# SyncE's transfers in the planner's order, and a table load that the planner counts

## The chip, the core and the metric

The kernel runs on one core of one Trainium2 chip. The core has five engines that run side by side: TensorE (PE in the profile) multiplies matrices, VectorE (DVE) and ScalarE (ACT) do elementwise work, GpSimd (POOL) does some elementwise work and issues accumulating transfers, and SyncE (SP) issues nearly all other transfers. Each engine works through its own list of instructions in order and waits on semaphores for the others. The metric is the device time of one execution in microseconds (us); less is better.

## The reference

Two layers of a decoder trunk work on one sequence of 512 tokens, with 16 learned tokens put ahead of it, so on 528 rows of width 1024, all in float32. Each layer has two halves, and each half is normalised before and after:

```python
for l in range(DEPTH):                      # DEPTH = 2
    u = rms_norm(h, mix_pre_g[l])
    z = u @ w_in[l]                         # q, k, v, forget gate, two conv groups
    y = concat(forgetting_attention(...),   # 8 heads of 64, causal, with a decay F[t] - F[s]
               conformer_conv(...),         # 31 taps, layer norm, silu, a pointwise matmul
               short_conv(...))             # 3 taps
    h += rms_norm(head_rms_norm(y) @ w_out[l], mix_post_g[l])
    u = rms_norm(h, ffn_pre_g[l])
    g, up = split(conv3(u @ w_up[l]))       # each 2816 wide, 3 taps along the sequence
    h += rms_norm((silu(g) * up) @ w_down[l], ffn_post_g[l])
return h[:, 16:]
```

## The kernel before, in words

**Layout.** Activations lie transposed: 128 channels on the partitions, 8 channel tiles (KD), 528 columns of sequence in two halves of 264. The last layer drops the first 16 columns, so most of its tiles are 512 wide in the FFN. To keep float32 accuracy every operand is split into a high and a low part (names ending in hi and lo), and each product is three matmuls: hi x hi, hi x lo, lo x hi (mm3, line 659 on, whose matmul is line 668; line 709 in the class First, lines 1204 and 1462 in the attention stages, line 2198 in the FFN).

**Weights** come in blocks through a ring of three raw buffers. For one block SyncE loads it (load in plan_block, line 604), ScalarE writes the high part (high, line 608), VectorE writes the low part (low, line 612), and then the raw buffer is free for the next load. In the FFN load_op (line 2061) loads the blocks of w_up into the buffers g and u, line 2336 those of w_down into draw and raw, and lines 2049 and 2052 split them.

**Stages of a layer.** The mixer (line 894) makes q, k, v and the convolution inputs, and runs the attention of head after head; small transfers by dma (line 535) copy rows of q and k and the gate rows of the heads (gate_rows, line 1270: from an SBUF tile for heads 0 to 3, from g_dram for heads 4 to 7). Then finish (line 1642) makes w_out, the norm and the addition to h; load_h (line 490) brings h back from DRAM for it. Then comes the FFN: 22 pairs of tiles f (NF), the first six by plain products, the other 16 by seven products in place of eight (class Seven, line 2066), whose operand sums GpSimd makes by accumulating transfers (line 2086). h is stored to h_mid for that time (line 1901). Each pair is filtered by three taps (conv_flow, line 2115), the gate half goes through silu (line 2151), the two are multiplied and split again (gate_flow, lines 2164, 2171 and 2175), and w_down is accumulated in five parts (downs, line 2318; the last part again by finish). Tile 21 is the last one, and the last part of w_down needs it last.

**What sets the order.** A planner written into the kernel (class Flow, line 247) decides it while the program is built. Each operation is given to it as engine, estimated duration, priority (lower goes first) and what it waits for; TensorE's work is given as threads. Flow.run (line 308) goes forward in estimated time: on each engine, among the operations that are ready by the time that it is free, the one of the lowest priority goes, and when an operation's turn comes, its instructions are emitted. An operation counts as ready 0.06 us (HOP) after what it waits for. So the planner has an order for every engine, SyncE among them ("sp" operations). In the program it holds only for the engines that manual_schedule names (the set every, line 1784): TensorE, ScalarE, VectorE and GpSimd. SyncE is left out of the set, and its transfers are put in order by the framework's own scheduler, which runs a simulated timeline over the program (the kernel is built with schedule_with_timeline_sim=True) and may take a transfer before others that were emitted earlier.

Priorities that matter here: the taps, silu and split of tile f have 1.5 + 0.001 f (conv_prio), the copies out of PSUM 0, blocks of w_up and w_down in the FFN about 1 + 0.001 f (part 0 of w_down 0.7 and 0.9, the plain blocks 0.5), the blocks of plan_block 2 unless something else is given, and the loads of h for the last finish of a layer 3, not before a time:

```python
plan_w(len(chunks) if final else after_mixer[l + 1])
h, h_at = load_h(fp, h_mid[l], prio=3, after_all=[Tok(flow.now + 4)])
```

**The table load.** ScalarE evaluates functions from tables. silu needs another set than the exponentials and logarithms of the norms and of the attention, so behind the last silu of a layer (f == NF - 1) the kernel loads the set EXPSET again (line 2154). In the planner the silu has act_us(n) = 0.17 + 0.0009 n us, and the table load nothing: it is emitted inside the silu's operation.

Of the kernel before, what the change touches and what calls it, by code (L numbers as in the profile page):

```python
# [26 lines left out]
NF = DFF // P  # L27
# [336 lines left out]
def act_us(n):  # L364
    return 0.17 + 0.0009 * n
# [6 lines left out]
def stt_us(n):  # L372
    return 0.22 + 0.00102 * n
# [13 lines left out]
def tile_hybrid_trunk(ctx: ExitStack, tc: tile.TileContext, xT, wflat, pv_d, out):  # L387
    nc = tc.nc
# [3 lines left out]
    def T(pool, shape, dt, tag, bufs=None):  # L392
        uid[0] += 1
        kw = {} if bufs is None else {"bufs": bufs}
        return pool.tile(list(shape), dt, tag=tag, name=f"{tag}_{uid[0]}", **kw)
# [4 lines left out]
    PE, ACT = mybir.EngineType.PE, mybir.EngineType.Activation  # L400
    DVE, POOL = mybir.EngineType.DVE, mybir.EngineType.Pool
# [67 lines left out]
    EXPSET = "natural_log_exp_and_others"  # L469
# [55 lines left out]
    def act(us, fn, *after, **kw):  # L525
        return flow.op("act", us, fn, after, **kw)

    def dve(us, fn, *after, **kw):
        return flow.op("dve", us, fn, after, **kw)

    def gp(us, fn, *after, **kw):
        return flow.op("pool", us, fn, after, **kw)
# [1248 lines left out]
    after_first = [next(i for i, c in enumerate(chunks) if c[0] == "ffn_w_up" and c[1] == l) + FIRST["w_out"] + 3  # L1781
                   for l in range(DEPTH)]
    after_down = next(i for i, c in enumerate(chunks) if c[1] == 1) + FIRST["ffn_w_down"]
    every = {PE, ACT, DVE, POOL}
    with tc.tile_pool(name="pre", bufs=2, reuse_waits="tile") as sp, tc.manual_schedule(engines=every):
        h, h_at = load_h(sp, xT, also=[(0, 2)], prios=OH)
        act(1.3, lambda: nc.scalar.preload_act_table_set(EXPSET), prio=-2)
# [21 lines left out]
    for l in range(DEPTH):  # L1809
        pv, pg = pvs[l]  # L1810
        final = l == DEPTH - 1
# [19 lines left out]
        with tc.tile_pool(name=f"fp{l}", bufs=2, reuse_waits="tile") as fp:  # L1831
# [47 lines left out]
            def wtap(i, t):  # L1879
                c = _COLS["ffn_w"] + 3 * t + i  # L1880
                return pv[:, c:c + 1]

            def z_of(f, e):
                return zs[(2 * f + e) % len(zs)]
# [159 lines left out]
            def split_op(box, name, raw, after, bufs, slot, n, prio):  # L2044


                def high():
                    box[name] = [t[:, :n] for t in bufs.get(slot)]
                    nc.scalar.copy(box[name][0], raw())  # L2049

                a = act(act_us(n), high, *after, prio=prio, takes=[(bufs.ring, slot)])
                return a, dve(dve_us(n), lambda: nc.vector.tensor_sub(box[name][1], raw(), box[name][0].bitcast(F32)), a, prio=prio)  # L2052

            def up_chunk(f, e):
                i = next(i for i, c in enumerate(chunks) if c[0] == "ffn_w_up" and c[1] == l and c[4][0][0] == e * DFF + P * f)
                return wflat[offs[i]:offs[i] + P * KD * P].rearrange("(p s) -> p s", p=P)

            def load_op(bufs, slot, box, name, src, n, prio):
                def load():
                    box[name] = bufs.get(slot)[:, :n]  # L2060
                    nc.sync.dma_start(box[name], src)

                return flow.op("sp", dma_us(n), load, prio=prio, lat=dma_lat(n), takes=[(bufs.ring, slot)])
# [48 lines left out]
            def conv_prio(f):  # L2112
                return (0.8 if f < N0 else 1.5) + 0.001 * f

            def conv_flow(f, e, after):

                t, z, n, box, slot = (f, NF + f)[e], z_of(f, e), 2 * fw, {}, Slot()

                def tap(i):
                    c = box["c"]  # L2120
                    if i == 2:
                        nc.scalar.activation(c, z[:, 2:2 + n], AF.Copy, scale=wtap(2, t))  # L2122
                    else:
                        nc.vector.scalar_tensor_tensor(c, in0=z[:, i:i + n], scalar=wtap(i, t), in1=c, op0=ALU.mult, op1=ALU.add)  # L2124

                def first_tap():
                    box["c"] = T(fp, [P, 2, H], F32, "c", 4).rearrange("p a b -> p (a b)")[:, :n]
                    tap(2)

                p = conv_prio(f)  # L2130
                a = act(act_us(n) + 0.06, first_tap, *after, prio=p, takes=[(c_ring, slot)])
                if f < NTAP:
                    third = Slot()

                    def scale():
                        box["t"] = T(fp, [P, 2, H], F32, "acc", 2).rearrange("p a b -> p (a b)")[:, :n]
                        nc.scalar.activation(box["t"], z[:, :n], AF.Copy, scale=wtap(0, t))

                    b = act(act_us(n) + 0.06, scale, *after, prio=p, takes=[(norms.acc, third)])
                    d = gp(ADD_US, lambda: nc.gpsimd.dma_start(box["c"], box["t"], accum_op=ALU.add), a, b, prio=p, lat=ADD_LAT)  # L2140
                    third.close(d)
                    tap_at.append(d)
                    a = dve(stt_us(n), lambda: tap(1), d, prio=p)
                    z_free[f, e] = [a, b]
                else:
                    for i in (1, 0):
                        a = dve(stt_us(n), lambda i=i: tap(i), a, prio=p)
                    z_free[f, e] = [a]
                if e == 0:
                    def silu():  # L2150
                        s = nc.scalar.activation(box["c"], box["c"], AF.Silu)
                        if f == NF - 1:
                            with tc.issue_after(s.ins):
                                nc.scalar.preload_act_table_set(EXPSET)

                    a = act(act_us(n), silu, a, prio=p)
                conv_at[f, e] = a, box, slot

            def gate_flow(f):
# [26 lines left out]
            def ups(units, bufs):  # L2186
# [36 lines left out]
                def p3(f):  # L2223
                    d, tok = yield from product(banks_of(f)[0], f, "s4", "b22", done[f, "u4"])
                    copied(f, "c12", 0, 1, d, tok)
                    conv_flow(f, 0, [done[f, "c11"], done[f, "c12"]])

                def p4(f):
                    d, tok = yield from product(banks_of(f)[1], f, "a22", "t4", done[f, "c22"])
                    less(f, "c21", 0, d, tok, done[f, "u2"])  # L2230
                    conv_flow(f, 1, [done[f, "c21"], done[f, "c22"]])
                    if f == NF - 1:
                        y_waits.extend(y_last)
                    gate_flow(f)
# [47 lines left out]
            def plain():  # L2282

                for f in range(2, N0):
                    for e in range(2):
                        tok, weights, held_by = plain_w[f, e]
                        slot = yield from flow.grab(pring[0]["mm"])
                        yield [tok]
                        ps, w = mmt(slot.buf), weights()
                        for k in range(KD):  # L2290
                            if f >= NU:
                                yield norm_at[k]
                            mm3({hf: ps[:, hf, :iws[hf]] for hf in range(2)}, w, [k], u_in, start=k == 0, stop=k == KD - 1)
                            tok = flow.mm(sum(3 * mm_us(n) for n in iws))
                            u_read[k] = [tok] if (f, e) == (NU - 1, 1) else None
                            if k < KD - 1:
                                yield
                        held_by.close(tok)
                        if (f, e) == (N0 - 1, 1):
                            last_plain.append(tok)  # L2300
                        t = z_of(f, e)
                        a = []
                        for hf, ((z, _), n) in enumerate(zip(i_spans, iws)):
                            dst, src = t[:, off + z - i0:off + z - i0 + n], ps[:, hf, :n]
                            waits = [tok, *z_free.get((f - 2, e), [])]
                            if f >= NU:
                                a.append(act(act_us(n), lambda dst=dst, src=src: nc.scalar.copy(dst, src), *waits, prio=0))
                            else:
                                a.append(dve(dve_us(n), lambda dst=dst, src=src, z=z, n=n: nc.vector.tensor_mul(
                                    dst, src, rz[:, z:z + n]), *waits, prio=0))  # L2310
                        slot.close(*a)
                        z_at[2 * f + e] = a
                        conv_flow(f, e, a)
                        yield
# [103 lines left out]
            with plan:  # L2418
# [10 lines left out]
                for f in range(2, N0):  # L2429
                    for e in range(2):  # L2430
# [6 lines left out]
                        a = load_op(bufs["g"], raw, box, "g", up_chunk(f, e), 2 * HALF, w)  # L2437
                        a = split_op(box, "w", lambda box=box: box["g"], [a], bufs["ghl"], slot, 2 * HALF, w)[1]
# [9 lines left out]
                for i in range(wpos[0], wpos[0] + 2):  # L2448
# [3 lines left out]
                    a = load_op(bufs["g"], raw, box, "g", src, n, 1.03)  # L2452
# [86 lines left out]
```

## Time and profile before

| | |
|---|---|
| median of 3 runs | 1271.86 us (1271.65 to 1276.69) |
| the profiled execution's own time | 1272.24 us |
| its span, first to last instruction | 1270.5 us |
| TensorE busy | 97% of the span |
| VectorE, ScalarE, GpSimd busy | 76%, 61%, 19% |
| mean granted TensorE clock | 0.995 of full speed |
| moved by transfers | 165.85 MB, 131 GB/s on average |

In the rows below, PE, DVE, ACT and POOL are TensorE, VectorE, ScalarE and GpSimd; SPq is SyncE issuing transfers; L604 is line 604. A row of a timeline has the start in us from the span's start, the duration in us, engine, line, operation, output<-inputs by the program's names, and in brackets how long the engine stood idle before it and what ended that. A row of waits has the total in us, the number of waits and the longest. The chain of waits is followed back from the last instruction: at each step to what released it.

### The profile page before, as it was taken

Reading aid. Unit: us, or ns where it says so; the run is one execution under the profiler, and the core shown is the slowest. Engines: PE = TensorE matmul, PEld = TensorE weight load, DVE = VectorE, ACT = ScalarE, POOL = GpSimd, SP = SyncE. Lnnn points to the kernel's source line nnn. Section 1 sums busy time; section 2 is a strip of 40 time slices with the busy share of each in tenths; the row PEclk is TensorE's granted clock in tenths of the full one; section 3 lists DMA queues with packets and bytes.
Section 4 is the critical chain, followed back from the end, with each engine's and each line's share of the span. In section 5 each row is a group of like instructions: output and inputs, shape, how many; then the busy total and the mean of one; then the engine's idle time right before and its main releaser. Section 6 shows DMA issues by size and latency. Waiting matters only on the chain.

```text
span 1270.5 us, 24515 instructions
## 1 busy us (share of the span) xinstructions
PE 1237.3 (97%) x9468; PEld 1187.7 (93%) x9468; DVE 969.2 (76%) x1752; ACT 775.3 (61%) x1571; POOL 236.4 (19%) x415
## 2 busy tenths in 40 slices
PE   8999999999999999999999999999998999999996
PEld 8999988999999999999999999889997999999996
DVE  7788877588866777778677888765897578778855
ACT  7257668667755555556673667685586565556552
POOL 1313321002122222120003233200022122112100
PEclk9999999999999999999999999999999999999998
DMA  6132231637486766776341322126376677668641
GB/s 226 51 102 60 63 89 34 218 113 169 106 194 139 191 160 147 170 162 184 114 141 35 95 80 68 56 74 206 128 171 144 155 163 170 165 146 180 142 142 67
DMA packets 73941, 165.85 MB, mean 131 GB/s; under 512 B 8080, under 2 KB 26640, under 8 KB 73312
## 3 DMA queue, kind: packets, MB, share of 16 engines
q1 hardware_dynamic: 52048, 124.86, 30.6%
q0 software_dynamic: 21360, 39.02, 18.9%
q8 instruction: 74, 1.21, 0.4%
q10 hardware_dynamic: 416, 0.40, 0.1%
q14 instruction: 43, 0.35, 0.1%
HBM read 129.14 MB, written 8.65 MB: 108 GB/s over the span
## 4 chain that ended last, share of the span: by engine, by line
PE 80%; DVE 6%; ACT 5%; DMA 5%; issue 3%; POOL 1%; SPq 0%; DVEq 0%; POOLq 0%; ACTq 0%
PE psum L668 37%; PE psum L2198 25%; PE psum L709 6%; PE psum L1204 4%; DMA raw<-in_w_dram 3%; PE psum L1462 2%; PE psum L1405 1%; PE psum L792 1%; DMA c<-acc 1%; PE psum L1361 1%; DVE wlo L612 1%; PE psum L1199 1%; DMA raw<-u 1%; POOL pf L1423 1%; ACT whi L608 1%
## 5 line engine op out<-in xcount | busy, mean ns | idle before, releaser
L668 PE MATMUL psum<-yhi,whi 128*128 128x264 f32 (+3 forms) x660 | 188.3, 300 | 3.1 <-ACT yp L2373 1.7
L668 PE MATMUL psum<-ylo,whi 128*128 128x264 f32 (+3 forms) x660 | 185.2, 295 | 1.1 <-DVE ylo L2175 0.8
L668 PE MATMUL psum<-yhi,wlo 128*128 128x264 f32 (+3 forms) x660 | 184.7, 295 | 0.1
L668 PE MATMUL psum<-uhi,whi 128*128 128x264 f32 (+1 forms) x640 | 165.1, 291 | 1.2 <-DVE q L1292 1.2
L668 PE MATMUL psum<-ulo,whi 128*128 128x264 f32 (+1 forms) x640 | 161.0, 284 | 0.1
L668 PE MATMUL psum<-uhi,wlo 128*128 128x264 f32 (+1 forms) x640 | 160.6, 283 | 0.0
L2124 DVE SCALAR_TENSOR_TENSOR c<-z,pv,c 128x528 f32<-128x528 f32 (+1 forms) x156 | 117.2, 758 | 29.3 <-ACT c L2122 26.5
L612 DVE TENSOR_TENSOR wlo<-raw,whi 128x1024 fp32r<-128x1024 f32 (+2 forms) x84 | 100.5, 1206 | 37.8 <-ACT whi L608 37.7
L668 PEld LDWEIGHTS psum<-yhi,whi 128*128 128x128 f32 x660 | 121.0, 189 | 8.4 <-ACT yp L2373 2.2
L668 PEld LDWEIGHTS psum<-ylo,whi 128*128 128x128 f32 x660 | 121.0, 189 | 4.4 <-DVE ylo L1088 1.1
L668 PEld LDWEIGHTS psum<-yhi,wlo 128*128 128x128 f32 x660 | 121.1, 189 | 3.2 <-DVE wlo L612 0.6
L668 PEld LDWEIGHTS psum<-uhi,whi 128*128 128x128 f32 x640 | 111.9, 188 | 4.3 <-issue 2.4
L668 PEld LDWEIGHTS psum<-ulo,whi 128*128 128x128 f32 x640 | 112.2, 188 | 0.5 <-DVE ulo L1947 0.3
L2211 ACT COPY z<-psum 128x264 f32<-128x264 f32 (+2 forms) x128 | 48.2, 377 | 105.4 <-PE psum L2198 104.7
L668 PEld LDWEIGHTS psum<-uhi,wlo 128*128 128x128 f32 x640 | 112.1, 188 | 0.0
L608 ACT CAST whi<-raw 128x1024 fp32r<-128x1024 f32 (+2 forms) x84 | 85.9, 1035 | 38.9 <-DMA raw<-in_w_dram 21.1
L937 DVE SCALAR_TENSOR_TENSOR cacc<-apad,pv,cacc 128x528 f32<-128x528 f32 x120 | 88.7, 768 | 0.3
L709 PE MATMUL psum<-uhi,whi 128*128 128x264 f32 (+1 forms) x320 | 85.0, 289 | 1.8 <-ACT uhi L840 1.8
L709 PE MATMUL psum<-uhi,wlo 128*128 128x264 f32 (+1 forms) x320 | 83.4, 283 | 0.0
L2052 DVE TENSOR_TENSOR wlo<-raw,whi 128x1024 fp32r<-128x1024 f32 (+4 forms) x78 | 76.6, 982 | 8.9 <-ACT whi L2049 8.3
L2049 ACT CAST whi<-raw 128x1024 fp32r<-128x1024 f32 (+4 forms) x78 | 66.4, 856 | 16.5 <-PE psum L668 10.3
L2198 PE MATMUL psum<-uhi,whi 128*128 128x264 f32 (+1 forms) x256 | 72.7, 284 | 2.2 <-ACT yp L2373 2.2
(317 smaller groups left out, 3729.2 us busy)
## 6 DMA issues: line engine op xcount, KB each, us to landing
raw<-in_w_dram SPq DMA_DIRECT2D x110, 512.0 KB
u<-in_w_dram SPq DMA_DIRECT2D x32, 512.0 KB
u<-in_w_dram POOLq DMA_DIRECT2D x32, 256.0 KB, 5.2
raw<-in_w_dram POOLq DMA_DIRECT2D x32, 256.0 KB, 4.0
u<-raw POOLq DMA_DIRECT2D x32, 256.0 KB, 3.8
raw<-u POOLq DMA_DIRECT2D x32, 256.0 KB, 4.4
raw<-in_w_dram SPq DMA_DIRECT2D x16, 448.0 KB
h_mid<-h SPq DMA_DIRECT2D x4, 1056.0 KB
```

The costliest lines, as they stand in the source:

```text
L608: nc.scalar.copy(box["hi"][:, :sz], box["raw"][:, :sz])
L612: nc.vector.tensor_sub(lo[:, :sz], box["raw"][:, :sz], box["hi"][:, :sz].bitcast(F32))
L668: nc.tensor.matmul(d, lhsT=w[a][:, k, cols], rhs=rhs(b, k, hf), start=start and i == 0 and p == 0, stop=stop and i == n - 1 and p == 2)
L709: nc.tensor.matmul(self.ps[hf, i], lhsT=self.ws[i].w[a][:, k, :], rhs=self.rhs(b, k, hf), start=k + a + b == 0, stop=k == KD - 1 and b == 1)
L937: nc.vector.scalar_tensor_tensor(conv[j], in0=src, in1=conv[j], scalar=col("a_dw_w", CK * j + i), op0=ALU.mult, op1=ALU.add)
L1204: nc.tensor.matmul(ps[:n, :nw], lhsT=(uhi, ulo)[ui][:, k, P * b:P * b + n], rhs=w[wi][:, k % 4, :], start=k == 0 and p == 0, stop=k == KD ...
L1462: nc.tensor.matmul(acc[:, s0 - qa:qz - qa], lhsT=vt[:, b].rearrange("p h d -> p (h d)")[:, o:o + P], rhs=pt, start=b == 0 and i == 0, stop ...
L2049: nc.scalar.copy(box[name][0], raw())
L2052: return a, dve(dve_us(n), lambda: nc.vector.tensor_sub(box[name][1], raw(), box[name][0].bitcast(F32)), a, prio=prio)
L2124: nc.vector.scalar_tensor_tensor(c, in0=z[:, i:i + n], scalar=wtap(i, t), in1=c, op0=ALU.mult, op1=ALU.add)
L2198: nc.tensor.matmul(d, lhsT=w[i][:, P * k:P * (k + 1)], rhs=terms[b][j][k](), start=start and k + p == 0, stop=k == KH - 1 and p == 2, skip ...
L2211: done[f, name] = act(us, lambda: nc.scalar.copy(z_of(f, e)[:, zin[h]], d[:, lo:]), *after, prio=0)
```

## The change

SyncE is added to the engines whose instructions stay in the order of emission. The table load behind the last silu is emitted without issue_after, directly behind the silu; and in the last layer (final) an operation of 1.28 us that emits nothing is given to the planner for ScalarE behind that silu, with a priority 1 below the silu's (so 0.521).

```diff
-    every = {PE, ACT, DVE, POOL}
+    every = {PE, ACT, DVE, POOL, mybir.EngineType.SP}
...
                     def silu():
                         s = nc.scalar.activation(box["c"], box["c"], AF.Silu)
                         if f == NF - 1:
-                            with tc.issue_after(s.ins):
-                                nc.scalar.preload_act_table_set(EXPSET)
+                            nc.scalar.preload_act_table_set(EXPSET)
 
                     a = act(act_us(n), silu, a, prio=p)
+                    if f == NF - 1 and final:
+                        act(1.28, lambda: None, a, prio=p - 1)
                 conv_at[f, e] = a, box, slot
```

## The prediction

> **What bounds the kernel now.** I read the page first, then the waits before TensorE's matmuls, then the chain of waits over the last 65 us, then TensorE, ScalarE, VectorE and SyncE there in order of time.
>
> ```profile
> span 1270.5 us, 24515 instructions
> PE 1237.3 (97%) x9468; PEld 1187.7 (93%) x9468; DVE 969.2 (76%) x1752; ACT 775.3 (61%) x1571; POOL 236.4 (19%) x415
> PE 80%; DVE 6%; ACT 5%; DMA 5%; issue 3%; POOL 1%; SPq 0%; DVEq 0%; POOLq 0%; ACTq 0%
> ```
>
> TensorE is busy for 97% of the span and holds 80% of the chain that ended last. An edit that moves neither matmul nor weight load can win only where TensorE stands still: in the start, in the attention stages, where VectorE and GpSimd release it, and in a few short gaps. Transfers hold 5% of the chain. The last of them stands right before TensorE's final run:
>
> ```profile
> 1213.97 1.04 DVE c L2124 x2
> 1215.01 5.65 DMA raw<-in_w_dram
> 1220.66 0.02 issue
> 1220.69 0.95 ACT whi L608
> ...
> 1221.66 1.09 DVE wlo L612
> 1222.75 0.61 DVE ylo L2175
> ...
> 1223.41 20.54 PE psum L668 x158
> 1243.95 0.86 PE psum L792 x4
> ```
>
> Time goes down the rows; the second number is how long each piece lasted. This is layer 1's last w_down. A weight block issued at 1215.01 takes 5.65 us to land, ScalarE splits it, VectorE makes its low half and only then ylo, the low half of the last gated tile, for which TensorE waits. TensorE itself:
>
> ```profile
> 1220.81 0.28 PE L668 MATMUL psum<-yhi,wlo 128*128 128x256 f32 x1
> 1222.20 0.38 PE L668 MATMUL psum<-yhi,whi 128*128 128x256 f32 x1 [1.11 <-ACT yhi L2171]
> 1223.41 0.38 PE L668 MATMUL psum<-ylo,whi 128*128 128x256 f32 x1 [0.83 <-DVE ylo L2175]
> ```
>
> Three starts lie 1.39 and 1.21 us apart, where 0.11 is the rule (3.5 us for 32, in the windows below): 2.6 - 2 x 0.11 = **2.4 us of standstill**. Its cause is on ScalarE and SyncE:
>
> ```profile
> 1213.64 0.93 ACT L608 CAST whi<-raw 128x896 fp32r<-128x896 f32 x1
> 1216.00 0.63 ACT L2151 ACTIVATE c<-c 128x512 f32<-128x512 f32 x1 [1.43 <-DVE c L2124]
> 1216.65 1.28 ACT L2154 ACT_TABLE_LOAD   x1
> 1217.94 0.94 ACT L608 CAST whi<-raw 128x896 fp32r<-128x896 f32 x1
> 1220.69 0.94 ACT L608 CAST whi<-raw 128x896 fp32r<-128x896 f32 x1 [1.80 <-DMA raw<-in_w_dram]
> 1221.53 0.61 ACT L2171 CAST yhi<-c 128x512 fp32r<-128x512 f32 x1
> ```
>
> ```profile
> 1181.52 0.33 SPq L604 DMA_DIRECT2D raw<-in_w_dram  x1
> 1194.25 0.33 SPq L2061 DMA_DIRECT2D raw<-in_w_dram  x1
> 1202.07 0.33 SPq L604 DMA_DIRECT2D raw<-in_w_dram  x1
> 1206.47 0.33 SPq L2061 DMA_DIRECT2D raw<-in_w_dram  x1
> 1212.54 2.36 SPq L490 DMA_DIRECT2D h<-h_mid  x4
> 1215.01 0.40 SPq L604 DMA_DIRECT2D raw<-in_w_dram  x1
> ```
>
> The planner did not know of the 1.28 us of line 2154, so it put the third whi ahead of yhi; its block was late, behind four loads of h; ScalarE, in order, waited 1.80 us on it, and yhi, whose input was long there, stood behind. The standstill has a tail, here in windows (busy time and count for PE, PEld, DVE, ACT and POOL, then the granted clock, DMA share and GB/s):
>
> ```profile
> 1224.30:1227.80 3.50, 3.50 (x19) 3.50 (x18) 2.38 (x3) 3.02 (x6) 0.00 (x0) 0.51 0.35 137
> 1228.00:1231.50 3.50, 3.50 (x32) 3.50 (x31) 1.09 (x1) 2.06 (x3) 0.00 (x0) 1.00 0.02 5
> ```
>
> After the gap the granted clock is 0.51 for 3.5 us and 19 matmuls go through where 32 do at 1.00: 3.5 x (1 - 19/32) = **1.4 us more**.
>
> **The change part by part.** The two edits in silu leave the instructions alone. The table load is emitted at the same place; ScalarE already runs in emission order, so the issue_after around it orders nothing that isn't ordered: 0. The empty step of 1.28 us, only in layer 1, alters the planner's clock alone, so up to the last silu all engines but SyncE keep their order. Behind it the planner sees ScalarE free 1.28 us later. Between silu and yhi lies the product:
>
> ```profile
> 1217.54 0.69 DVE L2164 TENSOR_TENSOR c<-c,c 128x512 f32<-128x512 f32 x1
> 1218.91 1.09 DVE L612 TENSOR_TENSOR wlo<-raw,whi 128x896 fp32r<-128x896 f32 x1 [0.69 <-ACT whi L608]
> ```
>
> The product ends at 1218.23. With silu, table, one whi and then yhi (priority 1.521 against 2), yhi runs at 1218.88 to 1219.49, and ylo behind the wlo of 1218.91 at about 1220.0 to 1220.7. TensorE wants yhi at 1220.93 and ylo at 1221.05, so both are there by 0.3 us. If another wlo (1.09) still came before ylo, some 0.8 us of the gap would stay. So the standstill is worth -2.4, from 0 (the order stays) to -2.4, and the half clock -1.4, all or nothing: it needs the gap. I take both whole: -3.8.
>
> SyncE's edit reaches the same gap by the other side. In the planner's order the block of 1215.01 (priority 2) stands ahead of the loads of h (priority 3, and not before four planner us). Its buffer is free when the low half of the block issued at 1206.47 is made, by the chain at 1213.97, so it goes 1.0 us earlier with no h ahead of it. Either edit alone would free yhi, so I don't add them. The loads of h come later by up to the wait for the next buffer, some 4 us; they are first read by the adds after the norm at 1243.95, 20 us on: 0. The loads of line 604 at 1181.52 and 1202.07 had been hoisted over the two of line 2061 and now follow 1206.47 directly, at about 1206.8 and 1207.2. With 5.65 us to land, the longest way shown here, the first is there at 1212.5, ahead of its whi at 1213.64: 0, with 1.2 us of cover; without cover the silu slips by the same amount.
>
> What is late next? The next blocks: the last group's 12 matmuls end at 1222.3 and two blocks of 21 matmuls (2.4 us each) at 1227.1, and the third block's low half is ready at 1222.75 even if it isn't earlier. Nothing takes the gap's place.
>
> Elsewhere SyncE's order changes in three kinds of places. (1) In the mixers:
>
> ```profile
> 136.52 11.44 SPq L535 DMA_DIRECT2D k<-g_dram  x4
> ```
>
> The gate rows k<-g_dram of later heads stand ahead of their emission and the queue waits on them; in the planner's order they go beside k<-k. What is queued behind is weights three blocks ahead of use, and no gap of TensorE there ends on a load: 0, from -0.5 to +1. (2) At the starts of finish and of the FFN the stores of h_mid and the loads of h change places with weights; their readers are over 10 us away: 0. (3) In the FFN the loads of u, of g and of w_down share the queue:
>
> ```profile
> SPq L2061 <- DMA raw<-u: 189.0, 30, 13.1
> ACT d0hi L2049 <- DMA draw<-in_w_dram: 11.4, 5, 3.0
> ```
>
> (us in total, times, longest.) The queue waits 30 times, 6.3 us each, for an accumulation before a load of u, and w_down stands behind; ScalarE waits for it 5 times, up to 3.0 us, without TensorE stopping. The planner's order is that in which ScalarE splits these blocks, so I take 0. Its bounds: downwards the idle before lines 668 and 2198 that ends on yp L2373,
>
> ```profile
> L668 PE MATMUL psum<-yhi,whi 128*128 128x264 f32 (+3 forms) x660 | 188.3, 300 | 3.1 <-ACT yp L2373 1.7 <-ACT yhi L2171 1.1 <-DVE yp L1660 0.2
> L2198 PE MATMUL psum<-uhi,whi 128*128 128x264 f32 (+1 forms) x256 | 72.7, 284 | 2.2 <-ACT yp L2373 2.2
> ```
>
> 1.7 + 2.2 = -3.9, if all of it were the loads' doing (the rows below show GpSimd's); upwards, +1.7 for each load that comes too late:
>
> ```profile
> 977.55 0.62 ACT L2049 CAST s4hi<-raw 128x512 fp32r<-128x512 f32 x1 [2.35 <-DMA raw<-u]
> 978.70 0.50 PE L668 MATMUL psum<-yhi,whi 128*128 128x512 f32 x1 [1.74 <-ACT yp L2373]
> ```
>
> **The sum:** -2.4 - 1.4 = -3.8 on the profiled execution's own 1272.24 (its span and 1.7 around it) gives 1268.4; that execution lies 0.4 above the median of the runs, so 1271.86 - 3.8 = **1268.1 us**.
>
> Two rules speak for less. The Trainium skill ("ScalarE: Activation LUTs", What ACT_TABLE_LOAD costs) gives a switch of set 1.28 us and a drain of about 1.38 more; the row above has the next CAST 0.01 us behind the load, so the trace shows no such drain. With it yhi would end at 1220.9 and ylo at about 1221.5, an estimate from that page, and half a microsecond of the gap would stay. The Trainium skill ("TensorE: Matmul & The Clock Gate", Part 1) has the clock fall to half after a whole idle window of some 3.4 us; here 2.4 us in two parts were enough. Were the half clock due to something else, the sum would be 1269.5.
>
> **The rivals.** *The order behind the silu stays*: ScalarE still splits the third block before yhi, because in the planner the product is late too, and the load gains only the 1.0 us. For it: the product ends 0.3 us behind the table load. Against it: a whi of 0.94 fills just that time. It gives 1272, at best 1270.5.
>
> *The queue blocks in the FFN* (slower): the planner's order sets loads of u, with their 6.3 us waits, ahead of loads that ScalarE needs first. ScalarE then stands in order, its copies to z and yp come late, and TensorE stops, 1.74 us at a time. It decides once a load is more than the 3.0 us late that ScalarE bears today. For it: the 30 waits, and the planner knows no DMA but by formula. Against it: today's queue waits the same way. Seven such stops, of 30 waits, and the 3.8 won: 1271.86 + 12.2 - 3.8 = 1280.
>
> *The loads were worth more*: the -3.9 above goes too: 1264.2. Against it: both stops come from copies behind ScalarE's own order and GpSimd's accumulations, which don't change.
>
> *Small losses in mixers and starts*: +2 to +6 on the sum, 1270 to 1274.
>
> **How the numbers follow.** The forecast (1266 to 1270) 0.55, the order stays 0.12, small losses 0.10, more won 0.10, the queue blocks 0.13. The range that leaves out no more than 0.2 reaches from 1264.8, most of the way to "more won", to 1275, over the small losses; the blocked queue lies outside. Half a per cent, about what a measurement of this kernel can tell from no change, is 6.4 us: faster means below 1265.5 (most of "more won" and a tail of the forecast) 0.12, slower above 1278.2 (most of the blocked queue) 0.12, within it 0.76.
>
> **What would show it.** Right: yhi of line 2171 starts before the third whi of line 608 behind the table load; TensorE has no gap over 0.5 us in the last 60 us; no window there with a clock near 0.5 before the final norm; the loads of line 604 stand ahead of those of h; the chain's DMA piece before the last run of line 668 is gone. Wrong: the gap between the last two gated products is still there, or idle before lines 668 and 2198 that ends on z, yp or d0hi grows by more than 2 us over the two FFNs.

## The result, and the profile after

| | before | after |
|---|---|---|
| median, same chip | 1271.76 us (6 runs) | 1281.14 us (1279.12 to 1282.12, 6 runs) |
| ratio to before | 1 | 1.0079, 95% interval 1.0062 to 1.0095 |
| profiled execution: span, own time | 1270.5, 1272.24 us | 1279.3, 1281.01 us |
| mean granted TensorE clock | 0.995 | 0.991 |

The kernel is slower by 0.8% (the two medians alone give 0.7%), where 1268.1 us and no measurable change were forecast. The page of after (shares of the chain; two groups of matmuls, whose columns are count | busy us, mean ns | idle us before it and what ended most of it):

```profile
PE 81%; DVE 5%; issue 5%; ACT 4%; DMA 4%; POOL 1%; SPq 0%; DVEq 0%; POOLq 0%; ACTq 0%
L668 PE MATMUL psum<-yhi,whi 128*128 128x264 f32 (+3 forms) x660 | 187.8, 299 | 0.8 <-ACT yp L2374 0.7
L668 PE MATMUL psum<-uhi,whi 128*128 128x264 f32 (+1 forms) x640 | 167.7, 295 | 10.6 <-DVE z L2310 9.3
```

The second group on the page of before:

```profile
L668 PE MATMUL psum<-uhi,whi 128*128 128x264 f32 (+1 forms) x640 | 165.1, 291 | 1.2 <-DVE q L1292 1.2
```

The shares of the chain hardly move. The second group does: TensorE now stands 9.3 us on z of line 2310 ahead of the plain products (lines behind 2154 have moved down by one). The gated products of w_down, which the prediction watched, stand for 0.8 us in place of 3.1.

**The end of the kernel went as forecast.** SyncE, ScalarE and the granted clock of after around the last w_down (timelines; then windows with busy time and count of PE, PEld, DVE, ACT and POOL, granted clock, DMA share, GB/s):

```profile
1219.30 7.43 SPq L604 DMA_DIRECT2D raw<-in_w_dram  x3
1226.78 1.97 SPq L490 DMA_DIRECT2D h<-h_mid  x4
```

```profile
1229.05 1.28 ACT L2153 ACT_TABLE_LOAD   x1
1230.34 0.94 ACT L608 CAST whi<-raw 128x896 fp32r<-128x896 f32 x1
1231.19 0.61 ACT L2172 CAST yhi<-c 128x512 fp32r<-128x512 f32 x1
1231.71 0.94 ACT L608 CAST whi<-raw 128x896 fp32r<-128x896 f32 x1
```

```profile
1228.00:1231.50 3.50, 3.50 (x32) 3.50 (x31) 2.81 (x5) 3.08 (x4) 0.00 (x0) 1.00 1.00 337
1231.50:1235.00 3.50, 3.44 (x30) 3.23 (x28) 3.24 (x5) 1.65 (x3) 0.00 (x0) 1.00 1.00 340
```

yhi runs behind one whi, the third block is the last of three that are issued ahead of h, and its whi waits for nothing. The clock stays at 1.00, and 32 and 30 matmuls go through where before had 19 in the window behind its gap. The same matmul that starts at 1220.81 in before, and the first products for the norm, which start there at 1243.95 (timeline, then chain, of after):

```profile
1233.21 0.28 PE L668 MATMUL psum<-yhi,wlo 128*128 128x256 f32 x1
1252.70 0.86 PE psum L792 x4
```

From one to the other it was 23.1 us and is now 19.5: 3.6 us are won.

**The loss is at the start of each FFN.** TensorE there, in layer 0 and in layer 1:

```profile
300.85 0.41 PE L668 MATMUL psum<-uhi,wlo 128*128 128x264 f32 x2
305.36 0.84 PE L668 MATMUL psum<-uhi,whi 128*128 128x264 f32 x2 [4.11 <-DVE z L2310]
...
932.46 0.40 PE L668 MATMUL psum<-uhi,wlo 128*128 128x250 f32 x2
938.08 0.84 PE L668 MATMUL psum<-uhi,whi 128*128 128x250 f32 x2 [5.23 <-DVE z L2310]
```

With 0.12 us for the second matmul of each first row and 0.11 for the usual distance, the standstills are 4.3 and 5.4 us, where before had none. What follows them, in windows:

```profile
304.50:308.00 3.50, 2.64 (x12) 2.67 (x13) 2.70 (x7) 3.19 (x4) 0.84 (x1) 0.50 1.01 315
308.00:311.50 3.50, 3.50 (x19) 3.50 (x19) 1.78 (x3) 1.26 (x2) 0.00 (x0) 0.56 1.11 271
...
936.00:939.50 3.50, 1.42 (x6) 1.45 (x7) 1.42 (x3) 2.63 (x4) 0.84 (x1) 0.50 1.05 324
939.50:943.00 3.50, 3.50 (x20) 3.50 (x19) 3.46 (x6) 2.40 (x5) 0.00 (x0) 0.57 0.41 73
```

At 32 matmuls in 3.5 us the busy times of these rows have room for 24, 32, 13 and 32; 12, 19, 6 and 20 went through. That is 12 + 13 + 7 + 12 = 44 matmuls at 0.11, so 4.8 us for the half clock. Together 4.3 + 5.4 + 4.8 = 14.5 us are lost there and 3.6 won at the end; the spans differ by 8.8. The other 2.1 are mostly short stops that come and go between executions (one of them is shown below).

**Whose lateness is it?** The chain of waits over that stretch of after, and the two accumulations of before:

```profile
293.31 10.67 DMA c<-acc
...
304.10 0.77 DVE c L2124
304.87 0.35 DVE z L2310
...
305.36 14.67 PE psum L668 x97
```

```profile
292.94 5.10 DMA c<-acc
...
299.18 6.13 DMA c<-acc
```

GpSimd's transfer c<-acc, the accumulation that adds one tap of the filter, takes 10.67 us in place of 5.10 (in layer 1 it takes 11.65). VectorE needs it for the next tap, in order ahead of z, and z gives TensorE its bank. SyncE beside it, in after and then in before:

```profile
282.25 0.33 SPq L2337 DMA_DIRECT2D draw<-in_w_dram  x1
291.78 0.33 SPq L2337 DMA_DIRECT2D raw<-in_w_dram  x1
292.16 0.90 SPq L1901 DMA_DIRECT2D h_mid<-h  x2
297.67 0.33 SPq L2061 DMA_DIRECT2D raw<-in_w_dram  x1
...
299.36 2.35 SPq L2061 DMA_DIRECT2D u<-in_w_dram  x2
```

```profile
273.69 6.01 SPq L1901 DMA_DIRECT2D h_mid<-h  x2
281.88 0.33 SPq L2336 DMA_DIRECT2D draw<-in_w_dram  x1
289.19 0.81 SPq L2061 DMA_DIRECT2D u<-in_w_dram  x2
291.42 0.33 SPq L2336 DMA_DIRECT2D raw<-in_w_dram  x1
```

Before, the stores of h_mid (1056 KB each) went out as h became ready, and the loads of u ahead of raw. In the planner's order draw (priority 0.7) and raw (0.71) come ahead of the stores (1), and both wait:

```profile
SPq L2337 <- PE psum L709: 22.2, 1, 22.2
SPq L2337 <- DVE wlo L612: 9.1, 1, 9.1
```

(us in total, times, longest.) The load of draw is given to the planner with its ring of buffers alone, so the planner doesn't know that it waits for line 709. SyncE, in order, holds the stores back until 292 us and the loads of u until 299. At 292 us GpSimd issues its accumulations, and the DMA engines are full in after, as they aren't in before (windows, after and then before):

```profile
295.00:300.00 5.00, 5.00 (x44) 5.00 (x43) 3.38 (x5) 1.68 (x2) 0.00 (x0) 1.00 1.04 368
```

```profile
295.00:300.00 5.00, 5.00 (x44) 5.00 (x43) 5.00 (x8) 4.07 (x5) 1.67 (x2) 1.00 0.71 175
```

The theory, then (A): the held-back bytes and the accumulations share the DMA engines. Its rivals: the loads behind draw do it and not the stores (B); ScalarE's changed order does (C); draw or what stands behind it comes late (D).

### The profile page after: what moved, and what is told of

The parts are those of the page before. It is cut to its first block, busy times and chain, and to the rows that moved or that the text cites. A ratio compares the mean times of both kernels' runs of the same rounds, so it can differ in the third digit from the quotient of the medians.

```text
span 1279.3 us, 24504 instructions
## 1 busy us (share of the span) xinstructions
PE 1240.8 (97%) x9468; PEld 1191.5 (93%) x9468; DVE 970.5 (76%) x1752; ACT 776.4 (61%) x1571; POOL 236.5 (18%) x415
## 4 chain that ended last, share of the span: by engine, by line
PE 81%; DVE 5%; issue 5%; ACT 4%; DMA 4%; POOL 1%; SPq 0%; DVEq 0%; POOLq 0%; ACTq 0%
PE psum L668 40%; PE psum L2199 24%; PE psum L709 5%; PE psum L1204 4%; PE psum L1462 2%; DMA c<-acc 2%; PE psum L1405 1%; PE psum L792 1%; DMA raw<-in_w_dram 1%; PE psum L1361 1%; PE psum L1199 1%; POOL pf L1423 1%; PE psum L1532 1%; POOL dm L1376 1%; DMA raw<-u 0%
```

## The experiments

Each ratio is to the kernel before on the same chip. No kernel below leaves out any of the computation.

**The table edit alone.**

```diff
-    every = {PE, ACT, DVE, POOL, mybir.EngineType.SP}
+    every = {PE, ACT, DVE, POOL}
```

> SyncE is left out of the manual order again; the edit of the table load stays. Theory A (the loss is SyncE's order alone, at the start of each FFN, where the stores of h_mid now stand behind two loads that wait): the two standstills of TensorE at 301 and 933 us are gone and the last w_down keeps yhi ahead of the third whi, so before's gap and half clock are gone: 1271.8 - 4.0 = 1267.8 us (1266.5 to 1269). Rival C (the loss comes with ScalarE's or the planner's changed order): the standstills stay, about 1281.

Measured: 1268.43 us, ratio 0.9982 (0.9968 to 0.9995), in the range, but by the ratio only 2.3 us are won, where 4.0 were expected (the kernel before took 1270.82 us on this chip). No standstill at the FFN starts: rival C is out, and the planner's step alone frees yhi. By the profile 2.9 of the 3.6 us are won at the end, since a smaller stop takes the gap's place:

```profile
1222.15 0.28 PE L668 MATMUL psum<-yhi,wlo 128*128 128x256 f32 x1
1223.21 0.39 PE L668 MATMUL psum<-yhi,whi 128*128 128x256 f32 x1 [0.77 <-DVE yp L1660]
```

Here the third block still stands behind h: ScalarE waits 1.17 us for it, its low half runs on VectorE ahead of yp, and TensorE waits for yp's bank. With SyncE in order that block is early, and this stop isn't there.

**The stores first.** An operation of 0 us emits them; the old one stays in the planner and emits nothing, so that nothing else moves.

```diff
+                def store(k0):
+                    nc.sync.dma_start(h_mid[l][:, k0:k0 + KH], h[:, k0:k0 + KH])
+                for k0 in (0, KH):
+                    flow.op("sp", 0, lambda k0=k0: store(k0), r_at, prio=0.6)
-                saved = [flow.op("sp", 2.7, lambda k0=k0: nc.sync.dma_start(...), r_at, lat=6.0)
+                saved = [flow.op("sp", 2.7, lambda k0=k0: None, r_at, lat=6.0)
```

> The changed kernel with one thing moved: both stores of h_mid are emitted ahead of the load of draw in each layer; no other engine and no other transfer changes its place. Theory A (the stores' 2.1 MB meet GpSimd's accumulations c<-acc on the DMA engines): the stores are issued near 273 and 900 us again, the accumulation that took 10.7 and 11.7 us takes about 5 to 6, TensorE's two standstills (4.3 + 5.4) and their half clock (2.6 + 2.1) vanish: 1281.1 - 14.4 = 1266.7 us (1265.5 to 1268.5). Rival B (it is the bunched loads of u and of the plain blocks, the stores add little): the accumulations stay near 10 us, the standstills stay, 1278 to 1281.

Measured: 1273.63 us, ratio 1.0020 (1.0006 to 1.0033). The standstills on z are gone, and 0.0079 - 0.0020 = 0.59% of the time, 7.5 us, with them: rival B as a whole is out. But 1266.7 was expected, so theory A in this form is not all. SyncE, the chain and TensorE's waits in layer 0:

```profile
298.59 1.33 SPq L2066 DMA_DIRECT2D u<-in_w_dram  x2
```

```profile
298.38 10.56 DMA c<-acc
```

```profile
PE psum L668 <- ACT uhi L1951: 0.9, 1, 0.9
PE psum L668 <- DVE ulo L1952: 0.8, 1, 0.8
```

The next accumulation now takes 10.56 us, where the one of 299.18 in before took 6.13. What runs beside it are the loads of u, 512 KB each, that before had issued at 289.19. ScalarE waits for the accumulation with uhi behind it, and TensorE stops on uhi and ulo.

**The stores between draw and the waiting load.** Their priority is WD0[l] + 0.005, and they keep their time in the planner; the waiting load of raw falls behind the next load of w_up by that.

> The changed kernel with both stores of h_mid one place forward: behind the load of draw, but ahead of the next load of raw, which waits until 291.8 and 923.6 us. Theory A (what counts is that the stores' bytes are through before GpSimd's first accumulations at 292 and 924): they are issued at about 282.6 and 914.4, need some 6 to 7 us, and are through by 289.5 and 921.5: no standstill, the same time as with the stores first, 1266.7 us (1265.5 to 1268.5). Rival D (they must be ahead of draw, because draw or the blocks behind it come late for ScalarE): the standstills stay in part, 1272 to 1281.

Measured: 1273.64 us, ratio 1.0026 (1.0013 to 1.0039): the same as with the stores first, though 1266.7 had been expected of both. The stores leave at 282.22, 10 us ahead of the accumulations. Rival D is out: the place ahead of draw doesn't matter, but being through by 292 does.

**One store first, one left.**

```diff
-                for k0 in (0, KH):
+                for k0 in (0,):
```

> The changed kernel with one of the two stores of h_mid (1.06 MB) ahead of the load of draw, the other left where the change puts it. Theory A (the delay goes with the bytes that meet the accumulations): 1.06 MB less is about 3 us at the 350 to 370 GB/s of that stretch, so the accumulation takes about 7.7 to 8.7 us, the standstills shrink from 4.3 and 5.4 to about 1.3 and 2.4 us, the half clock behind the first perhaps goes: 1270 to 1275 us. Rival B (the loads, not the stores): 1278 to 1281. Rival E (any store in that place stops the queue for as long): 1279 to 1282.

Measured: 1276.09 us, ratio 1.0041 (1.0028 to 1.0054), between the two and a little above the range, which had been built on 1266.7. The time of the accumulations goes with the bytes beside them. The first pair of accumulations of layer 0 (count, KB each, median us from issue to landing) with both stores first, with one late and with both late:

```profile
c<-acc POOLq DMA_DIRECT2D x2, 264.0 KB, 4.0
```

```profile
c<-acc POOLq DMA_DIRECT2D x2, 264.0 KB, 6.8
```

```profile
c<-acc POOLq DMA_DIRECT2D x2, 264.0 KB, 10.0
```

Each store of 1.06 MB costs about 3 us: that is about its time at the 368 GB/s of the window above. TensorE's standstill in layer 1 is 1.6 us with one late, 5.4 with both; in layer 0 it is 0.4 in place of 4.3.

The loss of time follows the bytes less evenly. Matched matmul by matmul with before, the two FFN starts cost about 6 us with both stores first, 8 with one late and 14 with both late: the first accumulations that land some 3 us later stop TensorE for only 0.4 and 1.6 us. With one late, 3.3 us more go between 1030 and 1200 us, against 0.6 and 0.5 in the profiles with both first and both late. Two stops of TensorE lie there (us in total, times, longest):

```profile
PE psum L668 <- DVE yp L2381: 1.4, 2, 0.8
```

No run says whether they belong to this order or come and go.

**The stores first and the first loads of u next** (f = 6 and 7, ahead of the waiting load of raw, by the same means).

```diff
-                    lu = load_op(bufs["u"], us, box, "u", src[1], 2 * HALF, w)
+                    lu = load_op(bufs["u"], us, box, "u", src[1], 2 * HALF, w, WD0[l] + 0.005 if f < N0 + 2 else None)
...
+                if early is not None:
+                    begun = flow.op("sp", 0, load, prio=early, takes=[(bufs.ring, slot)])
+                    return flow.op("sp", dma_us(n), lambda: None, [begun], prio=prio, lat=dma_lat(n))
```

> The kernel with both stores of h_mid first, and beside them the two loads of u for the first tiles by seven products (f = 6 and 7) ahead of the second load of w_down's first part, which waits until 291.6 us; nothing else changes its place. Theory A2 (every large transfer that SyncE holds back behind that waiting load then meets GpSimd's accumulations; with the stores first it was the loads of u that did, 298.6 to 299.9 us, and the accumulation behind them landed at 309 us): TensorE's stops at 312 to 315 and 941 us (2.7 + 1.1 - 0.8 and 1.6 + 0.4 + 0.8 us against the kernel with the table edit alone) vanish: 1273.6 - 5.8 = 1267.8 us (1266 to 1269). Rival B2 (what is left against the table edit alone comes from SyncE's order in the mixers or in the middle of the FFN): no change, 1272 to 1274.

Measured: 1268.19 us, ratio 0.9987 (0.9977 to 0.9997). The loads of u cost 1.0020 - 0.9987 = 0.33%, 4.2 us. With these four transfers (two stores, two loads) moved in each layer and all the rest of SyncE in the planner's order, the whole loss is gone. Rival B2 is out.

**The stores first, and once more in their late place.**

> The kernel with both stores of h_mid first, and the same stores written once more at the place where the change has them, behind draw and the waiting load of raw (2.1 MB more in each layer, the same data). Theory A (the bytes on the DMA engines beside the accumulations are the cost): the standstills before z at 301 and 933 us and their half clock come back, 1273.6 + 7.5 = 1281 us (1279.5 to 1282.5). Rival F (what counts is that the first store is done late: a buffer, a semaphore, the place in the queue): it stays at 1273.6 (1272.5 to 1275).

Measured: 1284.04 us, ratio 1.0107 (1.0091 to 1.0123), above the range that was expected. TensorE stands again, at the same two places:

```profile
304.74 0.66 PE L668 MATMUL psum<-uhi,whi 128*128 128x264 f32 x2 [3.84 <-DVE z L2315]
...
939.52 0.83 PE L668 MATMUL psum<-uhi,whi 128*128 128x250 f32 x2 [5.43 <-DVE z L2315]
```

Here the early stores have been made already. What moves beside the accumulations is the cause, not the lateness of a store or of what waits for it. Whether the bytes count or the number of packets isn't shown: a second store adds both.

**SyncE in order in the start and the mixers alone.**

```diff
-            plan.enter_context(tc.manual_schedule(engines=every))
+            plan.enter_context(tc.manual_schedule(engines=every - {mybir.EngineType.SP}))
```

> SyncE in the planner's order in the start and in the mixers alone; in finish and the FFN it is left out as before; the edit of the table load stays. The prediction's term for the mixers was 0 (-0.5 to +1): the same time as the table edit alone, 1268.4 us (1267.5 to 1269.5), and no stop of TensorE over 0.5 us in the attention stages that isn't there already. Rival G (the gate rows or q and k come later for the heads): 1270 to 1273.

Measured: 1268.24 us, ratio 0.9986 (0.9978 to 0.9995), the same as the table edit alone: the mixers' term is 0. The two kernels have the same order in the FFN, and yet their stop before the second plain product of layer 1 differs; first the table edit alone, then this one:

```profile
978.62 0.50 PE L668 MATMUL psum<-yhi,whi 128*128 128x512 f32 x1 [1.65 <-ACT yp L2374]
```

```profile
977.44 0.50 PE L668 MATMUL psum<-yhi,whi 128*128 128x512 f32 x1 [0.67 <-ACT yp L2374]
```

So the 1.0 us that after seems to win at this stop (0.68 in place of the prediction's 1.74) needs no change of order to appear.

**The change without the planner's empty step.**

```diff
-                    if f == NF - 1 and final:
-                        act(1.28, lambda: None, a, prio=p - 1)
```

> The changed kernel without the planner's empty step of 1.28 us: the third whi is ahead of yhi again, and its block is issued ahead of the loads of h. By the prediction (each of the two edits alone frees yhi): the same as the changed kernel, 1281.1 us (1280 to 1282). Rival H (SyncE's order brings the block only 1.0 us earlier, so 1.4 of the 2.4 us at the last w_down stay, and the half clock with them): 1281.1 + 1.4 + 1.4 = 1283.9 us (1282.5 to 1285).

Measured: 1282.91 us, ratio 1.0105 (1.0087 to 1.0122). The time lies outside the 1280 to 1282 expected and within rival H's range, but the interval overlaps that of the whole change (1.0062 to 1.0095), so the time alone doesn't decide. The gap at the last w_down:

```profile
1235.28 0.38 PE L668 MATMUL psum<-ylo,whi 128*128 128x256 f32 x1 [0.46 <-DVE ylo L2174]
```

The row before starts at 1234.53: 0.6 us are left of 2.4, and the clock behind it is 1.00. By this profile rival H (1.4 us and the half clock stay) is too much, and no loss at all too little. The spans differ by 1.9; only 0.8 of that is at the last w_down, the rest in the start, where this execution ran at a clock of 0.51 from 15 to 22 us and the other at 1.00.

## Why the prediction was wrong, step by step

- **The last w_down: -2.4 and -1.4.** Right. yhi is ahead of the third whi, the third block ahead of h, the gap and its half clock are gone: 3.6 by the profile, against 3.8. "Either edit alone would free yhi" held in the main: the table edit alone left a new stop of 0.9 us, SyncE's order alone left 0.6. "Nothing takes the gap's place" was true only of both together. Of the marks set for the last 60 us, two gaps of 0.5 and 0.6 us remain that before has too.
- **Elsewhere (1), the mixers: 0.** Right (0.9986 against 0.9982).
- **Elsewhere (2), the stores of h_mid at the starts of the FFN: "their readers are over 10 us away: 0".** This is the step that failed. The readers are indeed far away, and none of them was late. A store that leaves later was priced by who reads it; what it would meet was not asked. The row of before that had the answer is not in the prediction: the stores at 273.69, in a stretch without accumulations, with two loads of weights behind them of which one waits for line 709. Measured: 0.59% of the time, 7.5 us, against 0.
- **Elsewhere (3), loads of u, g and w_down in the FFN: 0 (-3.9 to +1.7 for each late load).** Wrong for the first two loads of u in each layer, by the same mechanism: 4.2 us. In the middle of the FFN 0 is right: with these and the stores moved, SyncE's order costs nothing (0.9987).
- **The rivals.** "The queue blocks in the FFN" had the time (1280) and the queue that waits. Its mechanism was another: it had loads come late for ScalarE, in seven stops of 1.74 us. What stopped TensorE twice, for 4.3 and 5.4 us with the half clock behind, was a transfer of GpSimd that stands in another queue and whose issue had not changed. "Small losses in mixers and starts" had the place, and +2 to +6 for it; it was 11.7.
- **The marks.** Idle before lines 668 and 2198 that ends on z and grows by more than 2 us was named as a sign of error, and it came: the 9.3 us of the page of after.

A rule of the Trainium skill ("DMA: Bandwidth & Descriptors", Issuing engines are not separate DMA queues) has transfers of the different issuing engines run on the same 16 DMA engines and interleave. The traces agree: 2.1 MB on SyncE's queue made a transfer on GpSimd's go from 5.10 to 10.67 us, at a DMA share of 1.04. So the order on one queue had to be priced for the transfers of the other as well, and the prediction didn't do that.

**A faster version.** Three kernels beat both, all alike within their intervals: the table edit alone (0.9982), that with SyncE's order in the mixers (0.9986), and the whole change with stores and loads of u moved (0.9987). The table edit alone is the simplest. Whether their differences of 0.05% are real stays open.

## What to carry to other kernels

A transfer that moves in its queue has two prices: who reads it, and whom it meets on the DMA engines at its new time; transfers of all queues have to be listed for that time, accumulations on the critical path first. When a queue is put into an order by priority, look for the first entry that waits for something the order doesn't know, and for the large transfers behind it: they will start in a bunch once it is released.

## What the runs showed of the hardware

The granted clock followed the standstills unevenly. After 4.3 and 5.4 us it was near 0.5 for about two windows of 3.5 us (0.50 and 0.56; 0.50 and 0.57). Two stops of 1.1 and 0.9 us within 2.5 us, with the stores first, were followed by half clock; two of 1.8 and 0.9 us within 3.2 us, with one store first, were not. The window behind each pair:

```profile
316.00:319.50 3.50, 3.50 (x18) 3.50 (x18) 3.50 (x5) 3.50 (x6) 0.00 (x0) 0.53 1.01 222
```

```profile
314.50:318.00 3.50, 2.21 (x14) 1.81 (x14) 3.44 (x5) 3.50 (x6) 0.96 (x2) 1.00 1.02 171
```

So the longer pair of stops kept the clock and the shorter one lost it. The Trainium skill ("TensorE: Matmul & The Clock Gate", Part 1) has activity judged in windows of about 3.4 us that run freely and don't start with the kernel. Where in a window a stop falls could then explain such a pair, but no run here shows the windows themselves; and in the shorter pair TensorE was never idle for a whole one.
